# A wider side copy, chained last sums in uneven pieces, and an earlier first load in a cosine-similarity kernel

## Chip, cores, metric

One core of a Trainium2 chip. The time of a kernel is the device time of one execution in microseconds (us); medians of several executions are quoted. The span of a profile (first to last instruction) is about 1.8 us shorter than the time of the same execution: 1250.0 us against 1251.8.

Names: SP issues the DMAs, ScalarE (ACT in the profile) squares and sums, VectorE (DVE) multiplies and sums, TensorE (PE) only transposes a few results at the end.

## The reference

```python
x, y: 8192 x 8192, float32
x_norm = norm(x, axis=1); y_norm = norm(y, axis=1)
return sum(x * y, axis=1) / (x_norm * y_norm + 1e-8)
```

Each row needs three sums: of x², of y² and of xy. 537 MB are read and 32 KB written.

## The kernel before

Rows go by 128. Thirty groups of 256 rows come first (an x load and a y load of 8.4 MB each), then four blocks of 128 rows, numbered 60 to 63. There are three slots of 64 KB per partition, so y of the next group can only be loaded once x of this group is done with. To free that slot sooner, VectorE copies the last `SIDE` columns of x into PSUM while it would be idle, and does the dot of those columns last.

```python
SIDE = 2560
...
for g in range(G):                                     # 30 groups
    cut = 2 * K - SIDE                                 # K = 8192
    square(xt[:, 0:K], ...); square(xt[:, K:], ...)    # ScalarE
    nc.vector.tensor_copy(out=side, in_=xt[:, cut:])
    dot(xt[:, 0:K], yt[:, 0:K], col(XY, c), xt[:, 0:K])        # result in place
    dot(xt[:, K:cut], yt[:, K:cut], part, xt[:, K:cut])        # after this, x's slot is free
    square(yt[:, 0:K], ...); square(yt[:, K:], ...)
    dot(side, yt[:, cut:], col(XY, c + 1), side, part)
    load(g + 1)                                        # x, then y; y takes the slot of this group's x
```

The products and squares themselves are never read; only their sums are. Yet each instruction writes them somewhere. ScalarE's go to `junk`, 8192 bytes per partition. VectorE's go in place over x where they are wide, and to `prod`, a PSUM tile, where they are narrow:

```python
for which, w, engine in pieces:                        # last four blocks
    ...
    if engine == "A":
        square(src, parts[:, q, i:i + 1], a)           # ScalarE, into junk[:, a:a+w]
    else:
        dot(src, src, parts[:, q, i:i + 1], prod[:, o:o + w])
    if which == "y":
        dot(xp, yp, parts[:, XY, i:i + 1], prod[:, o:o + w] if w <= SIDE else xp)
```

## Time and profile before

| what | value | where it is read |
|---|---|---|
| time, three executions | 1251.83 us (1251.70 to 1252.41) | timing |
| DMA, 31 to 1203 us | 100% busy, 433 GB/s | busy time by stretch |
| first load issued / first packet starts | 0.74 / 1.78 us | timeline, packet records |
| last input landed / last store issued | 1244.88 / 1247.77 us | semaphore records, timeline |
| VectorE / ScalarE busy | 52% / 73% | the page, part 1 |

The page's first line and its rows for the DMA engines, 40 equal slices of the span: busy tenths, then GB/s.

```profile
span 1250.0 us, 889 instructions
DMA  9999999999999999999999999999999999999998
GB/s 403 436 436 436 436 436 436 436 434 432 428 428 426 436 436 436 436 436 436 434 432 436 432 430 424 432 436 434 434 432 428 434 430 430 434 436 436 424 424 328
```

There is no slice where the DMA engines rest until the last. (A slice counts a packet where it starts, so its value jumps by a packet or two; over 1172 us the mean is 433.) The kernel is bound by one stream of loads. What can be saved is time before the stream starts, dear packets within it, and the work behind the last landing.

### The profile page before, as it was taken

How to read it: one execution, taken by the hardware profiler on the slowest of the kernel's cores; microseconds unless marked ns; L12 is line 12 of the kernel's file. 1: busy time of each engine (PE TensorE's matmuls, PEld its weight loads, DVE VectorE, ACT ScalarE, POOL GpSimd, SP SyncE). 2: the span in 40 equal slices, each digit the busy share in tenths (PEclk: the TensorE clock that was granted, in tenths of full speed). 3: DMA queues.
4: the chain of work that ended last, by engine and by line, in shares of the span. 5: the costliest groups of instructions: out<-in, count | busy, mean ns of one | idle time of the engine just before them, and what ended most of it. 6: DMA issues, size and time to landing. Idle time of an engine off the chain costs nothing.

```text
span 1250.0 us, 889 instructions
## 1 busy us (share of the span) xinstructions
PE 1.0 (0%) x3; PEld 0.2 (0%) x3; DVE 654.2 (52%) x252; ACT 917.1 (73%) x287; POOL 0.7 (0%) x6
## 2 busy tenths in 40 slices
PE   0000000000000000000000000000000000000000
PEld 0000000000000000000000000000000000000000
DVE  0544466444664446654456543565445654446566
ACT  3686776867868768677686776866867768677887
POOL 0000000000000000000000000000000000000000
DMA  9999999999999999999999999999999999999998
GB/s 403 436 436 436 436 436 436 436 434 432 428 428 426 436 436 436 436 436 436 434 432 436 432 430 424 432 436 434 434 432 428 434 430 430 434 436 436 424 424 328
DMA packets 11868, 536.97 MB, mean 430 GB/s; under 512 B 1331, under 2 KB 1365, under 8 KB 2645
## 3 DMA queue, kind: packets, MB, share of 16 engines
q1 hardware_dynamic: 11861, 536.91, 99.5%
q14 instruction: 7, 0.06, 0.0%
HBM read 536.87 MB, written 0.03 MB: 430 GB/s over the span
## 4 chain that ended last, share of the span: by engine, by line
DMA 62%; DVE 35%; ACT 1%; issue 1%; PE 0%; SPq 0%; DVEq 0%; ACTq 0%
DMA yg<-in_y_dram 59%; DVE xg L101 34%; DMA b<-in_y_dram 3%; ACT junk L97 1%; DVE b L101 1%; DVE prod L101 0%; DVE den L140 0%; DVEq L101 0%; DVE part L101 0%; DVE parts L101 0%; ACT norm L132 0%; DVE res L141 0%; SPq L68 0%; PE psl L186 0%; PE ps L147 0%
## 5 line engine op out<-in xcount | busy, mean ns | idle before, releaser
L101 DVE CUSTOM_DVE_ANT_0 xg<-xg,yg 128x8192 f32<-128x8192 f32 (+1 forms) x60 | 439.1, 7356 | 497.5 <-DMA yg<-in_y_dram 497.5
L97 ACT ACTIVATE junk<-xg 128x8192 uint8<-128x8192 f32 x60 | 421.8, 7029 | 167.8 <-DMA xg<-in_x_dram 166.8
L97 ACT ACTIVATE junk<-yg 128x8192 uint8<-128x8192 f32 x60 | 421.8, 7030 | 154.4 <-DMA yg<-in_y_dram 153.4
L118 DVE COPY side<-xg 128x2560 f32<-128x2560 f32 x30 | 84.8, 2828 | 72.7 <-DMA xg<-in_x_dram 72.7
L101 DVE CUSTOM_DVE_ANT_0 side<-side,yg,part 128x2560 f32<-128x2560 f32 x30 | 86.8, 2893 | 1.1
L97 ACT ACTIVATE junk<-b 128x8192 uint8<-128x8192 f32 (+7 forms) x20 | 57.5, 2877 | 6.0 <-DMA b<-in_y_dram 5.2
L101 DVE CUSTOM_DVE_ANT_0 b<-b 128x8192 f32<-128x8192 f32 (+1 forms) x4 | 26.2, 6553 | 12.8 <-DMA b<-in_y_dram 10.7
L101 DVE CUSTOM_DVE_ANT_0 prod<-b 128x768 f32<-128x768 f32 (+4 forms) x9 | 11.4, 1263 | 2.3 <-DMA b<-in_y_dram 2.2
L97 ACT ACTIVATION_READ_ACCUMULATOR junk<-yg 128x1 f32 x60 | 11.2, 186 | 0.0
L97 ACT ACTIVATION_READ_ACCUMULATOR junk<-xg 128x1 f32 x60 | 11.2, 186 | 0.0
L101 DVE DVE_READ_ACCUMULATOR2_ANT sums<- 128x1 f32 x62 | 6.9, 111 | 0.0
L97 ACT ACTIVATION_READ_ACCUMULATOR junk<-b 128x1 f32 x20 | 3.7, 186 | 0.0
L138 DVE TENSOR_TENSOR den<-norm 128x60 f32<-128x60 f32 (+1 forms) x2 | 0.4, 190 | 5.4 <-ACT norm L132 5.4
L101 DVE DVE_READ_ACCUMULATOR2_ANT part<- 128x1 f32 x30 | 2.5, 82 | 0.0
L92 ACT ACT_TABLE_LOAD x1 | 1.3, 1283 | 0.7 <-PEq L203 0.7
L147 PE MATMUL ps<-ident,res 128*30 128x128 f32 x2 | 0.6, 395 | 1189.4 <-DVE res L141 1189.4
L101 DVE DVE_READ_ACCUMULATOR2_ANT parts<- 128x1 f32 x11 | 1.4, 130 | 0.0
L93 ACT ACT_TABLE_LOAD x1 | 1.3, 1283 | 0.0
L132 ACT ACTIVATE norm<-sums 128x120 f32<-128x120 f32 (+2 forms) x3 | 0.7, 228 | 0.4 <-DVE sums L176 0.4
L140 DVE RECIPROCAL den<-den 128x60 f32<-128x60 f32 (+2 forms) x3 | 0.9, 289 | 0.1
L148 DVE COPY orow<-ps 30x128 f32<-30x128 f32 x2 | 0.5, 280 | 0.6 <-PE ps L147 0.6
L141 DVE TENSOR_TENSOR res<-sums,den 128x60 f32<-128x60 f32 (+2 forms) x3 | 0.5, 181 | 0.1
(15 smaller groups left out, 3.1 us busy)
## 6 DMA issues: line engine op xcount, KB each, us to landing
b<-in_x_dram SPq DMA_DIRECT2D x2, 4096.0 KB, 22.5
b<-in_y_dram SPq DMA_DIRECT2D x2, 4096.0 KB, 31.8
b<-in_x_dram SPq DMA_DIRECT2D x2, 2048.0 KB, 30.4
b<-in_y_dram SPq DMA_DIRECT2D x2, 2048.0 KB, 30.5
b<-in_x_dram SPq DMA_DIRECT2D x1, 1280.0 KB, 28.8
b<-in_y_dram SPq DMA_DIRECT2D x1, 1280.0 KB, 31.5
b<-in_x_dram SPq DMA_DIRECT2D x1, 1024.0 KB, 33.5
b<-in_y_dram SPq DMA_DIRECT2D x1, 1024.0 KB, 30.7
```

The lines of the kernel that those rows point to most:

```text
L92: nc.scalar.memzero(dummy)
L93: nc.scalar.sqrt(out=dummy, in_=dummy)
L97: nc.scalar.activation(out=junk[:, at:at + src.shape[-1]], in_=src, func=ACTF.Square, accum_out=acc)
L101: nc.vector.tensor_tensor_reduce(out=into, in0=a, in1=b, scale=1.0, scalar=init, op0=ALU.mult, op1=ALU.add, accum_out=acc)
L118: nc.vector.tensor_copy(out=side, in_=xt[:, cut:])
L132: nc.scalar.activation(out=norm[:, :, c], in_=sums[:, 0:2, c], func=ACTF.Sqrt)
L138: nc.vector.tensor_mul(out=den[:, c], in0=norm[:, 0, c], in1=norm[:, 1, c])
L140: nc.vector.reciprocal(out=den[:, c], in_=den[:, c])
L141: nc.vector.tensor_mul(out=res[:, c], in0=sums[:, XY, c], in1=den[:, c])
L147: nc.tensor.transpose(out=ps, in_=res[:, j:2 * G:2], identity=ident)
L148: nc.vector.tensor_copy(out=orow[:, :, j], in_=ps)
```

## The change

Four parts: 4096 instead of 2560 columns are copied aside, so x's slot is freed sooner. The first load is issued before the barrier that the engines hold at the start. The last two blocks come in 14 pieces instead of 18, uneven ones, and the last sums are chained: all but the last piece are reduced early, and the last dot starts from that sum. In the last four blocks VectorE's unneeded results no longer go in place over x or to `prod`, which took the copy's place in PSUM; all of them go to `junk`, which grows to 11264 bytes and becomes a ring for both engines: `room` hands out its bytes one result after the other and starts again at 0 when the next does not fit.

```diff
-    SIDE = 2560
+    SIDE = 4096
+    JUNK = K + 3072
...
+    nc.at_finalize(lead_with_first_load)      # moves the first DMA ahead of SP's Drain of the barrier
...
-        nt - 2: [("x", 4096, "A"), ("y", 4096, "A"), ("x", 4096, "A"), ("y", 4096, "A")],
-        nt - 1: [("x", 2560, "A"), ("y", 2560, "A"), ... 14 pieces, the last of 512],
+        nt - 2: [("x", 8192, "A"), ("y", 4096, "A"), ("y", 4096, "A")],
+        nt - 1: [("x", 4096, "V"), ("y", 3584, "A"), ("x", 2432, "A"), ("y", 1152, "A"),
+                 ("y", 1152, "A"), ("x", 1024, "V"), ("y", 896, "A"), ("y", 768, "A"),
+                 ("x", 640, "A"), ("y", 256, "V"), ("y", 384, "A")],
...
-    junk = junkpool.tile([P, K], U8, tag="junk")
+    junk = junkpool.tile([P, JUNK], U8, tag="junk")
...
+    def room(w):
+        a = ring[0] if ring[0] + w <= JUNK else 0
+        ring[0] = a + w
+        return a
...
-                square(src, parts[:, q, i:i + 1], a)
+                square(src, acc, room(w))
             else:
-                dot(src, src, parts[:, q, i:i + 1], prod[:, o:o + w])
+                r = room(w)
+                dot(src, src, acc, junk[:, r:r + w])
             if which == "y":
-                dot(xp, yp, parts[:, XY, i:i + 1], prod[:, o:o + w] if w <= SIDE else xp)
+                r = room(w)
+                dot(xs[b][:, a:a + w], src, xy, junk[:, r:r + w], init)
...
-    finish(last, nt)                          # reduce, root, 1/(..), product, transpose, copy, store
+    (root of the chained sums; the sum and 1/(..) transposed apart and multiplied; store)
```

More of the change, by code (lines that the diff above doesn't have):

```diff
@@ L16, with lead_with_first_load @@
 XX, YY, XY = 0, 1, 2
+def lead_with_first_load(nc):
+    blocks = nc.m.functions[0].blocks
+    opening, body = blocks[0], blocks[1]
+    load = next(i for i in body.instructions if i.opcode == "DMACopy")
+    assert not load.sync_info.on_wait
+    rest = [i for i in body.instructions if i.name != load.name]
+    head = list(opening.instructions)
+    at = next(n for n, i in enumerate(head) if i.opcode == "Drain" and i.engine == load.engine)
+    head.insert(at, load)
+    body.instructions = rest
+    opening.instructions = head
 @with_exitstack
@@ L36 @@
     G = (nt - NB) // 2
-    SIDE = 2560
+    SIDE = 4096
+    BANK = 512
+    JUNK = K + 3072
     xg = x[0:G * 2 * P, :].rearrange("(g p j) k -> g p (j k)", p=P, j=2)
@@ L47 @@
         nt - 3: [("x", 8192, "A"), ("y", 8192, "A")],
-        nt - 2: [("x", 4096, "A"), ("y", 4096, "A"), ("x", 4096, "A"), ("y", 4096, "A")],
-        nt - 1: [("x", 2560, "A"), ("y", 2560, "A"), ("x", 2048, "A"), ("y", 2048, "A"),
-                 ("x", 1280, "A"), ("y", 1024, "A"), ("x", 768, "V"), ("y", 768, "A"),
-                 ("x", 512, "A"), ("y", 768, "A"), ("x", 512, "V"), ("y", 512, "A"),
-                 ("x", 512, "A"), ("y", 512, "A")],
+        nt - 2: [("x", 8192, "A"), ("y", 4096, "A"), ("y", 4096, "A")],
+        nt - 1: [("x", 4096, "V"), ("y", 3584, "A"), ("x", 2432, "A"), ("y", 1152, "A"),
+                 ("y", 1152, "A"), ("x", 1024, "V"), ("y", 896, "A"), ("y", 768, "A"),
+                 ("x", 640, "A"), ("y", 256, "V"), ("y", 384, "A")],
     }
@@ L86 @@
     den = small.tile([P, nt], FP32, tag="den")
-    res = small.tile([P, nt], FP32, tag="res")
     ident = small.tile([P, P], FP32, tag="ident")
     dummy = small.tile([P, 1], FP32, tag="dummy")
-    junk = junkpool.tile([P, K], U8, tag="junk")
+    junk = junkpool.tile([P, JUNK], U8, tag="junk")
     nc.scalar.memzero(dummy)
@@ L132, in finish, with store_groups @@
         nc.scalar.activation(out=norm[:, :, c], in_=sums[:, 0:2, c], func=ACTF.Sqrt)
-        if b - a == 1:
-            nc.vector.tensor_scalar(
-                out=den[:, c], in0=norm[:, 0, c], scalar1=norm[:, 1, c], scalar2=EPS,
-                op0=ALU.mult, op1=ALU.add)
-        else:
-            nc.vector.tensor_mul(out=den[:, c], in0=norm[:, 0, c], in1=norm[:, 1, c])
-            nc.vector.tensor_scalar_add(out=den[:, c], in0=den[:, c], scalar1=EPS)
+        nc.vector.tensor_mul(out=den[:, c], in0=norm[:, 0, c], in1=norm[:, 1, c])
+        nc.vector.tensor_scalar_add(out=den[:, c], in0=den[:, c], scalar1=EPS)
         nc.vector.reciprocal(out=den[:, c], in_=den[:, c])
-        nc.vector.tensor_mul(out=res[:, c], in0=sums[:, XY, c], in1=den[:, c])
-    def store_groups():
+    def store_groups(ps):
+        c = slice(0, 2 * G)
+        res = small.tile([P, 2 * G], FP32, tag="res")
+        nc.vector.tensor_mul(out=res, in0=sums[:, XY, c], in1=den[:, c])
         orow = small.tile([G, P, 2], FP32, tag="orow")
         for j in range(2):
-            ps = psumpool.tile([G, P], FP32, tag=f"ps{j}", name=f"ps{j}")
-            nc.tensor.transpose(out=ps, in_=res[:, j:2 * G:2], identity=ident)
-            nc.vector.tensor_copy(out=orow[:, :, j], in_=ps)
+            nc.tensor.transpose(out=ps[j], in_=res[:, j:2 * G:2], identity=ident)
+            nc.vector.tensor_copy(out=orow[:, :, j], in_=ps[j])
         nc.sync.dma_start(
@@ L151, in store_groups @@
             in_=orow.rearrange("g p j -> g (p j)"))
+    tail = psumpool.tile([P, SIDE], FP32, tag="side", name="tail")
+    pst = [tail[0:G, j * BANK:j * BANK + P] for j in range(2)]
+    psl = [tail[0:NB, j * BANK:j * BANK + P] for j in range(2, 4)]
+    ring = [0]
+    def room(w):
+        a = ring[0] if ring[0] + w <= JUNK else 0
+        ring[0] = a + w
+        return a
     last = nt - 1
     for b, pieces in PIECES.items():
-        n = sum(1 for q in pieces if q[0] == "x")
-        assert n == sum(1 for q in pieces if q[0] == "y")
@@ L157 @@
-        if n > 1:
-            parts = small.tile([P, 3, n], FP32, tag=f"parts{b}", name=f"parts{b}")
-            prod = psumpool.tile([P, SIDE], FP32, tag="side", name=f"prod{b}")
-        else:
-            parts = sums[:, :, b:b + 1]
+        nx = sum(1 for q in pieces if q[0] == "x")
+        ny = len(pieces) - nx
+        parts = sums[:, :, b:b + 1]
+        if ny > 1:
+            m = max(nx, ny - 1 if b == last else ny)
+            parts = small.tile([P, 3, m], FP32, tag=f"parts{b}", name=f"parts{b}")
+            nc.vector.memzero(parts)
@@ L162 @@
+        if b == last:
+            base = small.tile([P, 3], FP32, tag="base")
+            fin = small.tile([P, 1], FP32, tag="fin")
         at, k = {"x": 0, "y": 0}, {"x": 0, "y": 0}
-        for which, w, engine in pieces:
+        for n, (which, w, engine) in enumerate(pieces):
             a, i = at[which], k[which]
             at[which], k[which] = a + w, i + 1
-            xp, yp = xs[b][:, a:a + w], ys[b][:, a:a + w]
-            src, q = (xp, XX) if which == "x" else (yp, YY)
-            o = SIDE - w if i % 2 else 0
+            src = (xs if which == "x" else ys)[b][:, a:a + w]
+            if b < last or n < len(pieces) - 1:
+                acc = parts[:, XX if which == "x" else YY, i:i + 1]
+                xy, init = parts[:, XY, i:i + 1], 0.0
+            else:
+                nc.vector.tensor_reduce(out=base, in_=parts, axis=AX.X, op=ALU.add)
+                acc, xy, init = fin, col(XY, last), base[:, XY:XY + 1]
@@ L169 @@
             if engine == "A":
-                square(src, parts[:, q, i:i + 1], a)
+                square(src, acc, room(w))
             else:
-                dot(src, src, parts[:, q, i:i + 1], prod[:, o:o + w])
+                r = room(w)
+                dot(src, src, acc, junk[:, r:r + w])
             if which == "y":
-                dot(xp, yp, parts[:, XY, i:i + 1], prod[:, o:o + w] if w <= SIDE else xp)
-        if n > 1:
+                r = room(w)
+                dot(xs[b][:, a:a + w], src, xy, junk[:, r:r + w], init)
@@ L176 @@
+        if ny > 1 and b != last:
             nc.vector.tensor_reduce(
@@ L179 @@
             finish(0, 2 * G)
-            store_groups()
+            store_groups(pst)
         if b == last - 1:
             finish(nt - NB, last)
-    finish(last, nt)
-    psl = psumpool.tile([NB, P], FP32, tag="ps0", name="psl")
+    nc.scalar.activation(out=norm[:, 0, last:], in_=base[:, XX:XX + 1], func=ACTF.Sqrt)
+    nc.scalar.activation(
+        out=norm[:, 1, last:], in_=fin, func=ACTF.Sqrt, bias=base[:, YY:YY + 1])
+    dots = small.tile([NB, P], FP32, tag="dots")
+    nc.tensor.transpose(out=psl[0], in_=sums[:, XY, nt - NB:], identity=ident)
+    nc.scalar.copy(out=dots, in_=psl[0])
+    nc.vector.tensor_scalar(
+        out=den[:, last:], in0=norm[:, 1, last:], scalar1=norm[:, 0, last:], scalar2=EPS,
+        op0=ALU.mult, op1=ALU.add)
+    nc.vector.reciprocal(out=den[:, last:], in_=den[:, last:])
+    nc.tensor.transpose(out=psl[1], in_=den[:, nt - NB:], identity=ident)
     orl = small.tile([NB, P], FP32, tag="orl")
-    nc.tensor.transpose(out=psl, in_=res[:, nt - NB:], identity=ident)
-    nc.vector.tensor_copy(out=orl, in_=psl)
+    nc.vector.tensor_mul(out=orl, in0=psl[1], in1=dots)
     nc.sync.dma_start(out=out.rearrange("(t p) -> t p", p=P)[nt - NB:, :], in_=orl)
```

## The prediction

> **What bounds it now.** The stream of loads. 536.87 MB pass in a 1250.0 us span. Busy time by stretch: from 31.25 to 1203.1 us the DMA engines are 100% busy at 433 GB/s; windows of 19.4 us read 427 to 434. From the first packet (1.78 us, packet records) to the last byte of input (1244.5) the packets' durations, divided by 16, fill the stretch without a hole. So only three things count: when the stream starts, what its packets cost, and what follows the last landing (1244.88; the last store is issued at 1247.77, the span ends 2.2 us later). The Trainium skill ("DMA: Bandwidth & Descriptors", Anatomy of one DMA) gives about 2.0 us fixed plus bytes at 436 GB/s, some 1233 us here; the trace's 433 decides.
>
> **4096 columns aside: about 0.** The dot before the release shrinks from 5632 to 4096 columns (6.02 to 4.43 us), so each y load is issued 1.6 us earlier. But it is issued 4.6 us before the x load ahead of it lands, and the stream has no gap there (433 GB/s across the hand-over). The copy grows from 2.83 to about 4.4 us in VectorE's idle time.
>
> **First load ahead of the barrier: -0.7 us.** SP issues it at 0.74 us, after a barrier released at 0.66; SP's own first instruction stands at 0.00. The first packet should start at about 1.0 instead of 1.78 us. As the stream never starves, all of it moves.
>
> **18 pieces for 22 in the last four blocks: -0.4 us.** Packets of 2 KB take 87 ns, of 64 KB 2420: 11 ns per packet beyond the bytes. 4 pieces x 8 packets per engine x 11.5 ns.
>
> **Tail: -0.3 us, the uncertain term.** Before, 2.89 us from last landing to store issue. After: reduction moved ahead of the last dot and chained as its start value, the product with the sum beside the reciprocal through a second transpose. Laying out the last block with this trace's costs (dot 0.08 to 0.2 + 1.04 ns a column, square 0.19 + 0.83 ns, operations of about 0.2) VectorE gets behind: it starts block 63's y pieces late after the block-62 norm and finishes the y256 dot 0.5 us after the last landing, reduces, ends the 384 dot near +1.4, then denominator, reciprocal, transpose, product: store at +2.6.
>
> **Prediction.** 1251.8 - 0.7 - 0.4 - 0.3 = 1250.4, with a little more likely from the tail, as these pieces look tuned: 1250.2 us, range 1249.0 to 1251.1. Faster by over 2%: 0.01; within 2%: 0.98; slower by over 2%: 0.01.
>
> **What would show it.** The first load's issue at about 0.0 in the timeline, first packets 0.7 earlier, x landing near 21.9 instead of 22.6. Bulk windows still 433 GB/s; y loads issued 1.6 us earlier with landings still 38.7 us a group apart. Last landing near 1243.7. In the chain of waits the end after the landing is VectorE (last dots, base, den), about 2.6 us to the store.
>
> **What would make it wrong.** SP's drain waiting for the load to land: all engines released only at 22 us, the second load late, a gap of some us. The early load slipping ahead of the span's zero, so that the time differs from this account. The 64 KB packets running longer in places, as they do by chance near 850 to 950 us (some 0.8 us in all before), hiding or feigning half the gain. VectorE's or ScalarE's backlog at the end being a us larger or smaller.

## More of the kernel before

All executions here are with a granted clock of 1.0.

The timeline of the kernel before in the last four blocks, cut to ScalarE's squares and VectorE's dots of blocks 60 and 61, from the square of y60 on (start, duration, engine, line, operation, out<-in, shapes, and in brackets the idle time before with what ended it):

```profile
1187.82 7.01 ACT L97 ACTIVATE junk<-b 128x8192 uint8<-128x8192 f32 x1
...
1190.18 8.67 DVE L101 CUSTOM_DVE_ANT_0 b<-b 128x8192 f32<-128x8192 f32 x1
...
1195.42 7.03 ACT L97 ACTIVATE junk<-b 128x8192 uint8<-128x8192 f32 x1 [0.49 <-DMA b<-in_x_dram]
...
1205.13 7.03 ACT L97 ACTIVATE junk<-b 128x8192 uint8<-128x8192 f32 x1 [2.59 <-DMA b<-in_y_dram]
1205.21 8.69 DVE L101 CUSTOM_DVE_ANT_0 b<-b 128x8192 f32<-128x8192 f32 x1 [6.35 <-DMA b<-in_y_dram]
```

The two engines work at the same time (1205.13 and 1205.21), and both wait for data. The waits of the same stretch, 1180 us to the end (who waited for whom: us in total, times, longest), say the same:

```profile
DVE b L101 <- DMA b<-in_y_dram: 10.7, 2, 6.4
...
ACT junk L97 <- DMA b<-in_y_dram: 5.2, 6, 2.6
...
DVE b L101 <- ACT junk L97: 2.1, 1, 2.1
```

VectorE waits for ScalarE once, for 2.1 us, because its result goes over x and the square of x must have read it first.

## The result

The changed kernel took 1263.62 us (1263.29 to 1263.95, 4 executions), the kernel before 1252.12 us (1251.70 to 1252.68). The ratio is 1.0092, with a 95% interval of 1.0074 to 1.0109. Such a ratio is the mean time of one kernel's fast runs over that of the other's of the same rounds, so it is not quite the ratio of the medians. The change makes the kernel slower by 11.5 us, or 0.9%: within the 2% that the prediction gave 0.98, and far outside its range in us.

The profile after, first the page:

```profile
span 1261.7 us, 874 instructions
DMA  9999999999999999999999999999999999999993
GB/s 432 432 432 432 432 432 432 432 432 432 432 432 432 432 432 432 440 438 436 438 434 434 432 433 432 432 432 432 432 432 434 432 432 432 432 432 431 432 423 147
```

The stream runs as before, and only the last slice is emptier (147 against 328 GB/s). The last input landed at 1243.72 us, earlier than before by 1.16. The last store was issued at 1259.71. So 16.0 us lie between the landing and the store, where 2.9 lay before: 13.1 us more behind the stream, less the 1.16 gained, gives the 11.94 us by which the store is later. The last store, before and then after:

```profile
1247.77 0.27 SPq L188 DMA_DIRECT2D out_dram<-orl  x1
```

```profile
1259.71 0.27 SPq L232 DMA_DIRECT2D out_dram<-orl  x1
```

Whatever went wrong is in the last blocks.

The same instructions of blocks 60 and 61 as shown of before, and the first two of block 62, in the timeline of the changed kernel:

```profile
1187.00 7.01 ACT L113 ACTIVATE junk<-b 128x8192 uint8<-128x8192 f32 x1
...
1194.14 8.69 DVE L117 CUSTOM_DVE_ANT_0 junk<-b 128x8192 uint8<-128x8192 f32 x1 [4.71 <-ACT junk L113]
...
1202.87 7.03 ACT L113 ACTIVATE junk<-b 128x8192 uint8<-128x8192 f32 x1 [8.77 <-DVE sums L117]
...
1210.02 7.03 ACT L113 ACTIVATE junk<-b 128x8192 uint8<-128x8192 f32 x1
...
1217.18 8.69 DVE L117 CUSTOM_DVE_ANT_0 junk<-b 128x8192 uint8<-128x8192 f32 x1 [14.34 <-ACT junk L113]
...
1225.91 7.03 ACT L113 ACTIVATE junk<-b 128x8192 uint8<-128x8192 f32 x1 [8.77 <-DVE sums L117]
...
1233.07 4.42 DVE L117 CUSTOM_DVE_ANT_0 junk<-b 128x4096 uint8<-128x4096 f32 x1 [7.19 <-ACT junk L113]
```

The engines take turns. VectorE's dot starts when ScalarE's square ends, the next square when the dot ends, and so on; every bracket names the other engine and none a DMA. The dot of block 61 starts at 1217.18 instead of 1205.21. The waits of the stretch from 1180 us to the end:

```profile
DVE junk L117 <- ACT junk L113: 26.2, 3, 14.3
ACT junk L113 <- DVE sums L117: 17.5, 2, 8.8
ACT norm L149 <- DVE sums L211: 5.9, 1, 5.9
```

VectorE waits for ScalarE 26.2 us where it waited 2.1, and ScalarE's squares for VectorE, which they did not before. (The third line is the norm of blocks 60 to 62, for which VectorE has the sums late.) What the two have in common there is `junk`. A result of 8192 bytes never fits behind another in a ring of 11264, so `room` puts every one of them at 0, on top of what the other engine has just written. Nobody reads it, but two writes to one place must keep their order, so the built program has a semaphore wait between them: the square of x61 waits there for VectorE's dot of block 60, where in the kernel before no square of these blocks waits for VectorE.

The early load did what it should. SP's timeline, the first two issues before and then after:

```profile
0.74 0.40 SPq L68 DMA_DIRECT2D xg<-in_x_dram  x1
1.20 0.42 SPq L70 DMA_DIRECT2D yg<-in_y_dram  x1
```

```profile
0.00 0.40 SPq L85 DMA_DIRECT2D xg<-in_x_dram  x1
0.81 0.35 SPq L87 DMA_DIRECT2D yg<-in_y_dram  x1
```

### The profile page after: what moved, and what is told of

The parts are those of the page before. It is cut to its first block, busy times and chain, and to the rows that moved or that the text cites. A ratio compares the mean times of both kernels' runs of the same rounds, so it can differ in the third digit from the quotient of the medians.

```text
span 1261.7 us, 874 instructions
## 1 busy us (share of the span) xinstructions
PE 1.3 (0%) x4; PEld 0.3 (0%) x4; DVE 705.1 (56%) x254; ACT 912.3 (72%) x279; POOL 0.7 (0%) x6
## 4 chain that ended last, share of the span: by engine, by line
DMA 62%; DVE 32%; issue 3%; ACT 2%; PE 0%; DVEq 0%; ACTq 0%
DMA yg<-in_y_dram 62%; DVE xg L117 30%; ACT junk L113 2%; DVE junk L117 2%; DVEq L117 0%; DVE part L117 0%; DVE parts L117 0%; ACT norm L149 0%; PE tail L223 0%; DVE sums L117 0%; PE tail L229 0%; DVE orl L231 0%; DVE den L151 0%; DVE base L200 0%; DVE den L150 0%
## 5 line engine op out<-in xcount | busy, mean ns | idle before, releaser
L117 DVE CUSTOM_DVE_ANT_0 xg<-xg,yg 128x8192 f32<-128x8192 f32 (+1 forms) x60 | 391.1, 6556 | 449.0 <-DMA yg<-in_y_dram 449.0
L134 DVE COPY side<-xg 128x4096 f32<-128x4096 f32 x30 | 132.8, 4427 | 71.4 <-DMA xg<-in_x_dram 71.4
L117 DVE CUSTOM_DVE_ANT_0 side<-side,yg,part 128x4096 f32<-128x4096 f32 x30 | 134.8, 4493 | 1.1
L113 ACT ACTIVATE junk<-b 128x8192 uint8<-128x8192 f32 (+8 forms) x15 | 53.0, 3535 | 17.7 <-DVE sums L117 17.5
L117 DVE CUSTOM_DVE_ANT_0 junk<-b 128x4096 uint8<-128x4096 f32 (+7 forms) x13 | 40.7, 3179 | 26.3 <-ACT junk L113 26.2
```

Source lines behind the costliest of these rows:

```text
L113: nc.scalar.activation(out=junk[:, at:at + src.shape[-1]], in_=src, func=ACTF.Square, accum_out=acc)
L117: nc.vector.tensor_tensor_reduce(out=into, in0=a, in1=b, scale=1.0, scalar=init, op0=ALU.mult, op1=ALU.add, accum_out=acc)
```

## The experiments

Theory A: the shared ring makes the two engines take turns, and this alone is the loss. Rival B: the uneven pieces leave the engines too much work behind the last landing. Rival C: the wider copy or the moved load upsets the stream. A fourth question came up on the way, theory D: what the side copy is really worth.

The first four ran on one chip beside the kernel before, at 1252.23 us (1251.71 to 1252.76, 9 executions).

### own_scratch: VectorE's results out of the ring

```diff
-                r = room(w)
-                dot(xs[b][:, a:a + w], src, xy, junk[:, r:r + w], init)
+                dot(xs[b][:, a:a + w], src, xy, vout(b, w), init)
                 # the same for VectorE's own squares; vout gives x of the block itself for
                 # blocks 60 and 61, and a ring over block 61's used x for 62 and 63
```

> The changed kernel with one edit: VectorE's unneeded results of the last four blocks go over x data that are already used (blocks 60 and 61 in place, 62 and 63 over block 61's x) instead of into the ring that ScalarE writes too. Theory A (the shared ring makes the two engines take turns, about 8.8 us of wait at a time): the 12.9 us of turns go, the last store is issued about 2.6 us after the last landing instead of 16.0, time 1250.3 us, range 1249.5 to 1251. Rival B (the uneven pieces leave the engines too much work after the last landing): time stays above 1258. Rival C (the 4096-column copy or the moved load upsets the stream): time stays above 1258 with the last landing later than before's.

Measured: 1250.32 us (1250.01 to 1250.72, 5 executions), ratio 0.9985 (0.9973 to 0.9998). The last input landed at 1243.92, the last store was issued at 1246.54, 2.62 us later. The dot of block 61, and the waits of its last stretch, 1180 us to the end:

```profile
1204.57 8.69 DVE L117 CUSTOM_DVE_ANT_0 b<-b 128x8192 f32<-128x8192 f32 x1 [6.36 <-DMA b<-in_y_dram]
```

```profile
DVE b L117 <- DMA b<-in_y_dram: 12.6, 3, 6.4
ACT junk L113 <- DMA b<-in_y_dram: 6.8, 3, 3.8
```

The two engines wait for data again. One edit that touches nothing but where unread results go takes away 13.3 us, all of the loss and more. (It also changes their type from uint8 to float32; a dot of 8192 columns takes 8.69 us either way.) B and C fall: pieces, copy and early load are all still in.

### before_shared_ring: the ring alone, in the kernel before

```diff
-                square(src, parts[:, q, i:i + 1], a)
+                square(src, parts[:, q, i:i + 1], room(w))
-                dot(xp, yp, parts[:, XY, i:i + 1], prod[:, o:o + w] if w <= SIDE else xp)
+                r = room(w)
+                dot(xp, yp, parts[:, XY, i:i + 1], junk[:, r:r + w])
                 # likewise VectorE's squares; ring of 11264 as in the change
```

> The kernel before with one edit: in the last four blocks ScalarE's squares and VectorE's dots take their places in one shared ring of 11264 columns, as the change has it; pieces, copy, start and end stay. Theory A: slower by 9 to 14 us, 1261 to 1266. Rivals B and C: 1252 within 1 us.

Measured: 1262.98 us (1262.25 to 1263.19, 4 executions), ratio 1.0084 (1.0069 to 1.0100): 10.8 us slower, by the ring and nothing else of the change. In the profiled execution the last landing came at 1245.87, 1.0 us later than in the kernel before, because some groups ran long ahead of the edited code; the store followed 13.2 us after it instead of 2.9, so the ring itself cost 10.3 us there. The same turns stand in its waits of the last stretch:

```profile
DVE junk L102 <- ACT junk L98: 25.7, 4, 14.3
ACT junk L98 <- DVE sums L102: 17.5, 2, 8.8
```

### wide_in_place: only the two widest results out of the ring

```diff
-                r = room(w)
-                dot(xs[b][:, a:a + w], src, xy, junk[:, r:r + w], init)
+                r = room(w) if w < K else None
+                into = xs[b] if w == K else junk[:, r:r + w]
+                dot(xs[b][:, a:a + w], src, xy, into, init)
```

> The changed kernel with only the two 8192-column dots of blocks 60 and 61 taken out of the ring (in place over x, as in the kernel before); the smaller results stay in the shared ring. Theory A in the form that nearly all is lost by the 8192-wide results, which leave no room for a neighbour in a ring of 11264: 1250.5 to 1253 us. If each small result waits as much as a wide one: 1255 to 1260. Rival B: no change, 1263.

Measured: 1252.32 us (1252.20 to 1252.82, 4 executions), 2.0 us over own_scratch. So 11.3 of the 13.3 us (1263.62 - 1252.32 and 1263.62 - 1250.32, across two sessions whose kernels before agree to 0.1) hang on two results, the dots of blocks 60 and 61. The other 2.0 come from one more meeting in the ring, as its timeline shows. The first dot of block 62 waits for the square of x62, which holds columns 0 to 8192:

```profile
1221.89 0.19 ACT L113 ACTIVATION_READ_ACCUMULATOR junk<-b 128x1 f32 x1
...
1222.11 4.43 DVE L117 CUSTOM_DVE_ANT_0 junk<-b 128x4096 uint8<-128x4096 f32 x1 [8.41 <-ACT junk L113]
```

In own_scratch this dot starts at 1219.38, when its data land. VectorE makes up only 0.7 of these 2.7 us: from the last landing to the last store it takes 4.64 us (1244.39 to 1249.03) instead of 2.62.

### before_early_load: the early load alone

```diff
+    nc.at_finalize(lead_with_first_load)               # and this function, as in the change
```

> The kernel before with the first load of x moved ahead of the opening barrier, nothing else. The stream of loads has no hole, so all of it moves: first packet at 1.0 instead of 1.78 us, last landing 0.7 us earlier, time 1251.4 us (0.7 less). If the head of the stream were hidden behind something else: no change.

Measured: 1251.46 us (1251.18 to 1251.90, 5 executions), 0.77 less than the kernel before in the same rounds. In its profile the last input landed at 1244.26 instead of 1244.88. The gain is that expected, though the interval of the ratio (0.9982 to 1.0007) is too wide to show it from the times alone.

The next four ran on one chip, beside the kernel before at 1252.10 us (1251.68 to 1252.94, 9 executions). Each takes the repaired kernel, own_scratch, and undoes or alters one part. Own_scratch itself ran on the chip of the first four, where the kernel before took 0.13 us more, so the differences below have at least that uncertainty; its repeat on a third chip (1250.20) lies as far below the kernel before, 1.91 us.

### own_no_early_load

```diff
-    nc.at_finalize(lead_with_first_load)
```

> The repaired kernel with the first load back behind the barrier. All in the stream moves back by 0.75 us: first packet 1.78, time 1251.1 us. If the early load is worth nothing in it: 1250.3.

Measured: 1250.88 us (1250.64 to 1251.02, 5 executions), 0.56 over own_scratch. First packet at 1.78 us, last landing 1244.41 instead of 1243.92. Both experiments on the load agree on 0.5 to 0.8 us.

### own_old_pieces

```diff
-        (the 14 new pieces of blocks 62 and 63)
+        (the 18 pieces of the kernel before)
```

> The repaired kernel with the 22 pieces of the kernel before in the last two blocks instead of the 14 new ones (22 against 18 in four blocks). By packet cost (11.5 ns a packet, 8 packets per engine and piece) the last landing comes 0.4 us later, 1244.3 instead of 1243.9. Time 1250.7 to 1251.3 us, according to how far the engines keep up with the smaller last pieces. If the pieces are what gained: over 1251.5; if they are worth nothing: 1250.3.

(The 22 are those of four blocks; the last two have 18 of them.)

Measured: 1250.60 us (1250.41 to 1250.66, 5 executions), 0.28 over own_scratch and just below the range expected. The last input landed at 1244.28, 0.36 later than in own_scratch: the cost of the packets, as reckoned. Part of it comes back: the store follows 2.36 us after the landing instead of 2.62, for a reason that was not traced. The new pieces are worth about 0.3 us.

### own_x4096_on_scalar

```diff
-        nt - 1: [("x", 4096, "V"), ...
+        nt - 1: [("x", 4096, "A"), ...
```

> The repaired kernel with the first piece of the last block (4096 columns of x) squared on ScalarE, idle there for 3.8 us, instead of VectorE, which runs about 0.2 us behind the landings from there to the end. Expected: last landing the same, from it to the last store 2.45 instead of 2.62 us, time 1250.2 us; too little to show in the times. If ScalarE then gets behind in its place: 2.6 us or more.

Measured: 1249.92 us (1249.83 to 1250.59, 5 executions), ratio 0.9983 (0.9970 to 0.9995). The last landing was at 1243.86 and the store at 1246.31, 2.44 us later, as expected to 0.01. It has the lowest median here. But the repeat of own_scratch, further below, took 2.49 us from landing to store where its first profile had 2.62, so a gain of the edit is shown neither by the times nor by the profile.

### own_copy_2560

```diff
-    SIDE = 4096
+    SIDE = 2560
```

> The repaired kernel (VectorE's results out of the shared ring) with 2560 instead of 4096 columns copied aside. If the copy's size is worth nothing in an undisturbed stream: 1250.3 us within 0.4, bulk windows 433 GB/s, y loads issued 1.6 us later with landings 38.7 us a group as before. If the earlier release did fill holes: slower by more than 0.5 us and a last landing later by as much.

Measured: 1251.03 us (1250.60 to 1252.04, 5 executions), 0.71 over own_scratch. That looked like a value of the copy. The profiled execution was the slowest, 1252.04, with the last landing at 1245.30 instead of 1243.92. The chain of work that ended last, cut to the y loads of some groups (start of the load's issue, us until it landed), first of the kernel before:

```profile
793.20 23.88 DMA yg<-in_y_dram
831.89 24.36 DMA yg<-in_y_dram
871.05 23.91 DMA yg<-in_y_dram
909.77 24.03 DMA yg<-in_y_dram
948.61 24.08 DMA yg<-in_y_dram
```

then of own_copy_2560:

```profile
792.99 23.88 DMA yg<-in_y_dram
831.68 24.53 DMA yg<-in_y_dram
871.01 24.44 DMA yg<-in_y_dram
910.25 24.05 DMA yg<-in_y_dram
949.11 23.89 DMA yg<-in_y_dram
```

and of own_scratch, with 4096 columns:

```profile
791.08 25.49 DMA yg<-in_y_dram
...
829.78 26.15 DMA yg<-in_y_dram
...
869.13 25.49 DMA yg<-in_y_dram
...
907.83 25.50 DMA yg<-in_y_dram
```

With 4096 columns every load of this stretch but one takes 25.49 or 25.50 us; the one near 830 is long in all the kernels with 2560 or 4096. With 2560 others are long as well, by 0.14 to 0.55 us. The packet records place the excess: these are first packets of y, which start 2 to 3 us after the y load's issue and take up to 4.4 us instead of 2.42. Hence theory D: what the copy buys is margin at the hand-over from an x load to the y load behind it, and 2560 columns are just about enough. The y load is issued 4.6 us before the x load ahead of it lands with 2560 columns, and 6.2 us before with 4096. (Ahead of this stretch, near 250, 290 and 750 us, groups run 0.05 to 0.63 us long with either size; that is not explained.)

The last three ran on one chip, beside the kernel before at 1252.11 us (1251.49 to 1253.46, 9 executions).

### own_copy_1024, own_scratch_again and own_copy_2560_again

```diff
-    SIDE = 4096
+    SIDE = 1024
-    tail = psumpool.tile([P, SIDE], FP32, tag="side", name="tail")
+    tail = psumpool.tile([P, 4 * BANK], FP32, tag="tail", name="tail")
```

(The edit of own_copy_1024; the other two are own_scratch and own_copy_2560 unchanged.)

> The repaired kernel with 1024 columns copied aside (and the transposes in a tile of their own, since theirs was the copy's). Each y load is then issued about 3.0 us before the x load ahead of it lands, instead of 4.6 with 2560 columns and 6.2 with 4096. Theory D (what the copy buys is margin at this hand-over: in the profiles with 2560 columns some engines' first packets of y ran 0.1 to 2 us long, 2 to 3 us after the issue, and single groups took 38.85 to 39.24 us instead of 38.70; with 4096 none did): with 1024 columns many groups go over 38.70, 0.2 to 1 us each, 5 to 25 us in all, 1255 to 1275 us. If the long packets have nothing to do with the hand-over: 1251.0 within 0.7, as with 2560.

> The repaired kernel again, beside the run with 1024 columns, on the same chip: 1250.3 us within 0.4, all groups from 780 to 1160 us of the profile 38.70 us apart but the one near 829 us, which runs long in every profile so far.

> The repaired kernel with 2560 columns again, beside the other two. Theory D: 1250.6 to 1251.6, slower than with 4096 by 0.3 to 1 us, with some groups after 780 us over 38.75. If the difference seen before was chance: within 0.2 us of the run with 4096 columns.

Measured with 1024 columns: 1278.58 us (1276.88 to 1279.86, 4 executions), ratio 1.0206 (1.0191 to 1.0222); with 4096: 1250.20 (1249.94 to 1250.26, 5); with 2560: 1250.67 (1250.47 to 1251.00, 5). The chain of own_copy_1024, cut to the y loads again:

```profile
811.85 22.89 DMA yg<-in_y_dram
...
851.14 24.73 DMA yg<-in_y_dram
...
892.27 24.41 DMA yg<-in_y_dram
...
933.08 22.66 DMA yg<-in_y_dram
```

The issues stand 39.29, 41.13 and 40.81 us apart instead of 38.70. Over 29 hand-overs the 28.4 us come to about 1 us each. The measured lead is 3.1 us. From 40 to 1160 us the DMA engines are 99% busy at 422 GB/s, where own_scratch has 100% and 433: they stand idle in part, besides the long packets. Theory D holds in its direction, and the loss is above its upper bound of 25.

The repeat with 2560 went half as expected. The difference in time is there (0.47 us), but not where I looked for it. In its profile no group after 780 us but the one near 830 is long, and the last landing, 1243.71, is that of own_scratch_again, 1243.66. The 0.47 us lie at the end: the store comes 2.97 us after the landing instead of 2.49. With a narrower tile for the transposes the built program makes the second transpose wait for ScalarE's copy of the first, a side effect of my edit:

```profile
1245.96 0.38 PE L236 MATMUL tail<-ident,den 128*4 128x128 f32 x1 [0.35 <-ACT dots L231]
```

In own_scratch_again it starts at 1245.37. Why the program gets this wait I have not found out. So some 0.4 us of both differences belong to the edit. The rest, the worth of 4096 against 2560 columns, is between 0 and 0.3 us in the medians; in one profiled execution of two it was 1.4 us (the landing), in the other 0.05. The packet records of all the profiles still bear theory D out. Counting packets of 64 KB that start within 7 us after a y load's issue and take over 3 us, the seven profiles with 4096 columns have none, the five with 2560 have 8 to 21, and the one with 1024 has 184. So in each profile with 2560 columns first packets of y run long at some hand-overs, the repeat included (11); but the last landing came about 1 us or more late in two of the five alone, own_copy_2560 and before_shared_ring.

## Why the prediction was wrong

It foresaw 1250.2 us, between 1249.0 and 1251.1; 1263.6 was measured.

- **What bounds the kernel: right.** One stream without a hole; the last landing, foreseen near 1243.7, came at 1243.72.
- **First load, -0.7: right.** The issue is at 0.00, the first packet at 1.02 instead of 1.78 us, the first square at 21.93 instead of 22.64. Alone it gave 0.77 us in the times, and taken out of the repaired kernel 0.56.
- **Fewer pieces, -0.4: right** for the landing (0.36 us); 0.28 in the time.
- **Wider copy, about 0: nearly right in its size, too sure in its reason.** The prediction called 4.6 us a lead at which nothing is lost. It is close to an edge: with 3.1 us of lead 28 us are lost, and at 4.6 one profiled execution lost 1.4 us in the landing and another 0.05. With 6.2 us no profile showed a first packet of y over 3 us.
- **Tail, -0.3: this step failed.** "Laying out the last block with this trace's costs" put the last store 2.6 us after the last landing; it came 16.0 after. The layout let ScalarE and VectorE each go on as soon as its data and its own last instruction allowed. It had no edge between the two for the ring, though the diff shows that both take their room from one counter, and in the built program the square of x61 waits for VectorE, which it does not in the kernel before. The prediction does not mention the move of the results into `junk` at all. It also laid out the last block only, from the block-62 norm on, while the loss builds up in blocks 60 and 61: there VectorE's dot of block 61 started 12.0 us later than before (1217.18 against 1205.21).
- With the ring taken away the same layout holds: 2.62 us foreseen as 2.6, and 1250.3 us in the range for 1250.2. Its steps hold too: the y256 dot ends 0.51 us after the last landing (foreseen 0.5) and the 384 dot 1.44 (1.4), so this is not luck. The costs were right and the dependence was missing. The terms sum to -1.4 us; the repaired kernel is 1.9 faster in the times and 1.5 in the profiled spans (1250.0 and 1248.5). Of the 1.5 in the spans, 0.96 are the earlier landing, 0.27 the tail and 0.25 what follows the store's issue (2.25 against 2.00 us), for which the prediction has no term; the rest in the times is of the size of the spread and not explained.

The method that finds such a loss is the Trainium skill's ("Perfetto Trace Analysis", Optimization Strategy): look for the gap on the engine and for the semaphore that it waits for. Here the gaps of 8.77 and 14.34 us named the other engine at once, and the trace agrees with the page that this leads to the cause.

## What to carry to other kernels

Where an instruction must write something that nobody reads, look at who else writes that place: a scratch shared by two engines is a lock between them, and a ring does not help when one result takes more than half of it. When laying out a stage by hand, take the waits from the built program first and the durations second. How early the next load is issued has an edge; a lead that seems to cost nothing may lie 1.5 us from it, as here, so try one step to the wrong side before calling it free.

## What the Trainium skill lacked or had wrong

- "DMA: Bandwidth & Descriptors", Where 436 GB/s comes from, says without a condition that for HBM to SBUF the HBM side binds at about 358 GB/s. With one core running, the stream from HBM went at 433 GB/s here. The page's own table of measurements has 425 for one core alone and keeps 358 for two; the sentence lacks that condition.
- The same page, Specifications, gives about 0.6 us to the first byte for a DMA issued from SP. From the start of the issue to the start of the first packet the trace has 1.02 to 1.04 us; counted from the end of the 0.40 us issue it agrees (0.62 and 0.64). It does not say from where it counts.
- The same page has a cost per packet for small ones alone, none for wide rows. Packets of 2 KB took 87 ns and of 64 KB 2420 ns, some 11 ns each beyond the bytes; 4 pieces less moved the last landing by 0.36 us.
- No page read says how early a load must be queued behind another for the stream to stay whole. Here 6.2 us before the landing of the load ahead was enough, 4.6 nearly always, and 3.1 us cost about 1 us at each of 29 hand-overs of 8.4 MB loads.
- No page read says that unread results in a shared scratch tie ScalarE and VectorE together. It cost 10.8 us alone in the kernel before, and 13.3 us in the changed kernel.
